# A hybrid layer on one core: ten ring tiles, square sums and scalings in quarters, and the first transfer on another queue

## The chip, the cores and the metric

The kernel runs on one core of a Trainium2 chip. The metric is the device time of one execution in microseconds (us); below, times inside the profiled execution count from the start of its span. TensorE (PE) multiplies, VectorE (DVE) and ScalarE (ACT) do element-wise work, GpSimd (POOL) does small work and issues its own transfers, SyncE (SP) issues transfers only. Each engine works through its instructions in order, and an instruction that waits holds all behind it.

## The reference

One layer over 256 rows of 2048 numbers, with two branches, all in float32:

```python
h = rms_norm(x, norm_g)
q, k, v, z_a, u_b, v_b, z_b, g_a, g_b = split(h @ w_in)      # 1024 columns each, g_a and g_b 2048
q, k = rms_norm of each head of 128, times its gain           # 8 heads
att = causal softmax attention(q, k, v)                       # one block: 256 rows are one MoBA block
y_a = (att * silu(z_a)) @ w_proj_a
sgu = gelu(u_b) * (causal w_spatial @ rms_norm(gelu(v_b), sgu_norm_g) + b_spatial)
y_b = (sgu * silu(z_b)) @ w_proj_b
out = x + (sigmoid(g_a) * y_a + sigmoid(g_b) * y_b) @ w_out
```

The sums of squares that concern the change are those of q and k and of gelu(v_b), each over groups of 128 columns.

## The kernel before

The weights are laid out in HBM as 120 tiles of 1 MB, 128 partitions of 2048 numbers, and one tile is one step i. Steps 0 to 7 make q, 8 to 15 k, then v, za, vb, ub, zb in eights (up to 55); from 56 on each of four column groups c has eight steps of the gates (g) and four of the projections (proj, PSUM tiles y); steps 104 to 119 make the output. A number after a tile's name is its step: tl13 is the tile tl of step 13.

Every float32 product is made from halves of fewer bits: ScalarE casts raw to wh, DVE subtracts to get wl (raw - wh), and TensorE does three products with the high and low halves. A plain step takes 24 matmuls. Of the eight steps of a projection behind q, up to five are Strassen steps (function `strassen`), which need 21 matmuls, and in exchange three more blocks: DVE makes t (lines 172 to 174, three instructions), ScalarE its high half th (L175), DVE its low half tl (L177). One of the four blocks of such a step is the sum of two, and this sum is made by transfers: SyncE copies a 256 KB piece of the weights to a ring of HBM tiles (L130, `pre_copy`), GpSimd adds a second piece by a transfer that accumulates (L134, `pre_sum`), and SyncE loads the ring tile as the first quarter of raw (L141) and the other 768 KB from the weights (L122). raw has four buffers, wh, wl and th three, tl two and t one.

The orders of SyncE and GpSimd are those in which the program is written (`queues`), so copies, loads, sums and GpSimd's powers stand in a fixed row. The orders of TensorE, DVE and ScalarE are found from step 8 on by the scheduler of the language, with costs of its own; up to there DVE and ScalarE go by the program too.

The loop over steps issues load(i + 3), pre_copy(i + 8), pre_sum(i + 6) and the split of step i + 2, then the matmuls of step i, then what `at` has put down for this step: `at(s, fn, ...)` calls fn at step s. `sums` squares a projection on ScalarE in four tiles of 128 x 512 (m, c), four instructions each with a sum along 128 columns (junk, ss); `rsqrt` makes the mean on DVE (ms, L268) and takes the power -0.5 on GpSimd (rs, L269); for k, DVE multiplies rs once more (L406). `norm_qk` and `norm_v` scale on ScalarE, four instructions for each tile (L415, L423). The tiles k_c11, k_c12, k_h, k_c22 are the four tiles of k.

At the start xv (the norm's gain and the first 256 columns of x transposed), raw0 in pieces and the rest of x are issued by SyncE in this order.

Of the kernel before, what the change touches and what calls it, by code (L numbers as in the profile page):

```python
# [12 lines left out]
F32 = mybir.dt.float32  # L13
# [3 lines left out]
AF = mybir.ActivationFunctionType  # L17
ALU = mybir.AluOpType
AX = mybir.AxisListType

P = 128
S = 256
# [7 lines left out]
B = 512  # L30
# [20 lines left out]
NVEC = KT + 2 + H  # L51
# [20 lines left out]
def hybrid_layer_kernel(  # L72
# [9 lines left out]
    nc = tc.nc  # L82
# [7 lines left out]
    small = ctx.enter_context(tc.tile_pool(name="small", bufs=4))  # L90
    psum = ctx.enter_context(tc.tile_pool(name="psum", bufs=1, space=bass.MemoryType.PSUM))
    dram = ctx.enter_context(tc.tile_pool(name="dram", bufs=1, space=bass.MemoryType.DRAM))
# [4 lines left out]
    def u(name, dtype=F32):  # L97
        return unit.tile([P, B], dtype, tag="u", name=name)
# [11 lines left out]

    raw, wh, wl, th, tl = {}, {}, {}, {}, {}
    pre = {}
    ring = [dram.tile([P, B], F32, tag=f"ring{n}", name=f"ring{n}") for n in range(6)]

    def strassen(i):
        if i >= NG or G[i][0] != "quad" or G[i][1] == G[0][1]:
            return False
        name, c, kp = G[i][1:4]
        return kp in SK or (name in FIVE and kp == 4) or (name == "g" and c in SIX and kp == 5)

    def load_piece(i, a, b):
        nc.sync.dma_start(raw[i][:, a:b], w[i, :, a:b])  # L122

    def new_raw(i):
        raw[i] = wpool.tile([P, WORDS], F32, tag="raw", bufs=4, name=f"raw{i}")

    def pre_copy(i):
        if i < NG and strassen(i):
            pre[i] = ring[len(pre) % len(ring)]
            nc.sync.dma_start(pre[i], w[i, :, 0:B])  # L130

    def pre_sum(i):
        if i in pre:
            nc.gpsimd.dma_start(pre[i], w[i, :, B:2 * B], accum_op=ALU.add)  # L134
# [44 lines left out]
    X = {}  # L179

    def heads(ap):
        return ap.rearrange("p (h d) -> p h d", d=P)
# [3 lines left out]
    xv = u("xv")  # L186
# [7 lines left out]
                          xT[:, NVEC + p0 * S:NVEC + p1 * S].rearrange("p (k t) -> p k t", t=S))  # L194

    new_raw(0)
    nc.sync.dma_start(xv[:, 0:NVEC + S], xT[:, 0:NVEC + S])
    load_piece(0, 0, B)
    load_piece(0, B, 2 * B)
    load_x(1, 2)  # L200
# [47 lines left out]
    gain = const.tile([P, P], F32, name="gain")  # L248
# [14 lines left out]
    rstd = const.tile([P, 2], F32, name="rstd")  # L263
    ssum = const.tile([P, 2], F32, name="ssum")

    def rsqrt(dst, src, n, count):
        ms = small.tile([P, 8], F32, tag="ms", name="ms")
        nc.vector.tensor_scalar(ms[:, :n], src, 1.0 / count, EPS, op0=ALU.mult, op1=ALU.add)  # L268
        nc.gpsimd.tensor_tensor(dst, ms[:, :n], mhalf[:, :n], op=ALU.pow)  # L269
# [121 lines left out]
        return [[c11, c12], [h, c22]]  # L391


    def sums(C, name):
        for m in range(2):
            for c in range(2):
                ss = small.tile([P, 4], F32, tag="ss", bufs=8, name="ss")
                junk = u("junk")
                scale = rstd[:, m:m + 1] if name == "k" else 1.0
                for h in range(4):  # L400
                    nc.scalar.activation(junk[:, h * P:(h + 1) * P], C[m][c][:, h * P:(h + 1) * P], AF.Square,
                                         scale=scale, accum_out=ss[:, h:h + 1])
                rs = small.tile([P, 4], F32, tag="rs", bufs=8, name="rs")
                rsqrt(rs, ss, 4, P)
                if name == "k":
                    nc.vector.tensor_scalar(rs, rs, scale, None, op0=ALU.mult)  # L406
                X["rs", name, m, c] = rs

    def norm_qk(name):
        C = X[name]  # L410
        for m in range(2):
            for c in range(2):
                for h in range(4):
                    sl = C[m][c][:, h * P:(h + 1) * P]
                    nc.scalar.activation(sl, sl, AF.Copy, scale=X["rs", name, m, c][:, h:h + 1])  # L415

    def norm_v():
        C = X["vb"]
        for m in range(2):
            for c in range(2):  # L420
                for h in range(4):
                    sl = C[m][c][:, h * P:(h + 1) * P]
                    nc.scalar.activation(sl, sl, AF.Copy, scale=X["rs", "vb", m, c][:, h:h + 1])  # L423
                t = heads(C[m][c])
                nc.vector.tensor_tensor(t, t, gain[:, None, :].to_broadcast([P, 4, P]), op=ALU.mult)

    def func(name, fn):
        for m in range(2):
# [168 lines left out]
    def at(i, fn, *a):  # L597
        later.setdefault(i, []).append((fn, a))
# [7 lines left out]
    i0 = first["q", 0]  # L606
# [6 lines left out]
    at(i0 + 6, halves_f, "x")  # L613
    at(i0 + 8, halves_4)
    i0 = first["k", 0]
    at(i0 + 1, sums, None, "q")
    at(i0 + 3, norm_qk, "q")
    i0 = first["v", 0]
    at(i0 + 0, turn_qk, "q", None)
    at(i0 + 1, sums, None, "k")  # L620
    at(i0 + 3, norm_qk, "k")
    i0 = first["za", 0]
    at(i0 + 0, turn_qk, "k", None)
    at(i0 + 1, score, None)
    at(i0 + 2, softmax, 0)
    at(i0 + 2, softmax, 1)
    i0 = first["vb", 0]
    at(i0 + 0, turn_p, 0, None)
    at(i0 + 0, turn_p, 1, None)
# [4 lines left out]
    i0 = first["ub", 0]  # L634
    at(i0 + 0, turn_z, "za", None)
    at(i0 + 0, causal_mix)
    at(i0 + 1, func, "vb", AF.Gelu_apprx_tanh)
    at(i0 + 2, sums, None, "vb")
    at(i0 + 4, norm_v)
    i0 = first["zb", 0]  # L640
    at(i0 + 0, mix, None)
    at(i0 + 1, func, "ub", AF.Gelu_apprx_tanh)
# [1 line left out]
    i0 = first["g", 0]  # L644
# [35 lines left out]
    for i, (kind, name, c, kp, n) in enumerate(G):  # L680
        if i == 8:
            ordered.close()
        if i:
            load(i + 3)
        if i >= 1:
            pre_copy(i + 8)
            pre_sum(i + 6)
        split(i + 2, 2 if i < 2 else 1)
        if i < 4:
            split_x(i + 4)  # L690
        plain = i < 8
        if kind == "quad":
            if n == 0:
                if i and G[i - 1][0] == "quad":

                    E, L = L, E
                Lt = [bank(b, f"acc_{name}{c}_{j}") for j, b in enumerate(L[:3])]
                Et = None
            if len(Lt) == 3 and (plain or not strassen(i)):
                Lt.append(bank(L[3], f"acc_{name}{c}_3"))  # L700
            if strassen(i) and Et is None:
                Et = [bank(b, f"seven_{name}{c}_{j}") for j, b in enumerate(E)]
            if strassen(i):
                last = SK[-1] if name not in FIVE else 5 if name == "g" and c in SIX else 4
                f8 = "m" if name == "out" else "x"
                seven(Et, Lt, i, kp, kp == SK[0], kp == last, n > 0, *fac(name), X["Fh", f8], X["Fl", f8])
                if kp == last:
                    e = early(Et, f"{name}{c}", xres.get(c) if name == "out" else None)
            else:
                direct(Lt, *fac(name), i, kp, (n == 0, not direct22(i)), n == 7)  # L710
            if n == 7:
                if plain:
                    X[name] = [[u(f"{name}{m}{j}") for j in range(2)] for m in range(2)]
                    for j in range(4):
                        nc.scalar.activation(X[name][j // 2][j % 2], Lt[j], AF.Copy, scale=rstd[:, j // 2:j // 2 + 1])
                elif name == "out":
                    post_out(c, Lt, e)
                elif name == "g":
                    X["g", c] = final(Lt, e)
                    for m in range(2):  # L720
                        for j in range(2):
                            nc.scalar.activation(X["g", c][m][j], X["g", c][m][j], AF.Sigmoid, scale=rstd[:, m:m + 1])
                else:
                    X[name] = final(Lt, e)
        elif kind == "proj":
            if n % 2 == 0:
                Y = (Y if n else []) + [bank(E[n + m], f"y{n}_{c}{m}") for m in range(2)]
            z = ("za", "zb")[n // 2]

            def hl(k, m):  # L730
                return (X[z + "h"][:, k, m * P:(m + 1) * P], X[z + "l"][:, k, m * P:(m + 1) * P])

            mm_rows(Y[n // 2 * 2:], hl, i, None, 4 * (n % 2), n % 2 == 0, n % 2 == 1)
            if n == 3:
                merge(c, Y)
        for fn, a in later.pop(i, []):
            a = list(a)
            if fn is sums:
                a[0] = X[a[1]]
            elif a and fn in (turn_qk, score, turn_p, attend, turn_z, mix, turn_m):  # L740
                if a[-1] is None:
                    a[-1] = list(E)
                    if fn is turn_p and a[0] == 1:
                        a[-1] = [E[3], E[0], E[1]]
                    if fn is attend:
                        a[-1] = E[2 * a[0]:]
                elif a[-1] == "late":
                    a[-1] = E[2:4] + L[0:2]
                elif a[-1] == "L01":
                    a[-1] = L[0:2]  # L750
                elif a[-1] == "L23":
                    a[-1] = L[2:4]
                elif a[-1] == "L3":
                    a[-1] = L[3:4]
            fn(*a)
# [48 lines left out]
```

## Time and profile before

| | before |
|---|---|
| median of 3 runs | 670.8 us (667.85 to 671.66) |
| profiled execution, time | 668.79 us |
| its span | 667.1 us |
| TensorE busy | 653.7 us (98%), 2959 matmuls |
| DVE busy | 601.8 us (90%) |
| ScalarE busy | 432.3 us (65%) |
| GpSimd busy | 73.2 us (11%) |
| mean granted TensorE clock | 0.997 |
| DMA engines, mean | 249 GB/s; HBM traffic 295 GB/s over the span |

The profiled execution spends 1.69 us outside the span. A busy share counts matmuls as running until their modelled ends, so a TensorE that is busy all the time may still wait a little between them. In a row of the timeline the first two numbers are the start and the duration of an instruction, or from the start of the first to the end of the last of a merged group (x2, x16); a bracket at the end gives the idle time of the engine just before, and what ended it.

### The profile page before, as it was taken

The page shows a single profiled execution, that of the slowest core. Times are in us where ns is not written, and L with a number is a line of the kernel's source. Part 1 is how long each engine was busy: PE and PEld are TensorE (multiplying, and loading weights), DVE is VectorE, ACT ScalarE, POOL GpSimd, SP SyncE. Part 2 cuts the span into 40 slices and gives each one's busy share as a digit, 9 for nine tenths or more (in the row PEclk, how much of TensorE's full clock was granted, in tenths as well). Part 3 has the DMA queues.
Part 4 walks back from the last instruction along what each step waited for, and adds up shares of the span by engine and source line. Part 5 has one row for each costly group of instructions (what it writes and reads, how often), then busy time and mean ns, then how long its engine had stood idle before and what let it go on. Part 6 is the DMA issues. An engine that isn't in the chain of part 4 may idle for free.

```text
span 667.1 us, 8042 instructions
## 1 busy us (share of the span) xinstructions
PE 653.7 (98%) x2959; PEld 533.4 (80%) x2959; DVE 601.8 (90%) x587; ACT 432.3 (65%) x521; POOL 73.2 (11%) x85
## 2 busy tenths in 40 slices
PE   8999899999999999999999999999999999999997
PEld 4888678788888788888877887788788878888875
DVE  4779888999898999999998999979988998999896
ACT  7968949857877679685654755556555564754360
POOL 1110503101000305000001100100010000000000
PEclk9999989999999999999999999999999999999999
DMA  8998894789687858967658973995598599777841
GB/s 303 396 407 272 257 333 145 208 282 271 176 284 219 257 201 251 329 194 235 220 205 271 283 250 145 340 289 199 194 350 249 204 276 307 242 181 246 235 200 63
DMA packets 47703, 166.28 MB, mean 249 GB/s; under 512 B 5296, under 2 KB 5936, under 8 KB 40112
## 3 DMA queue, kind: packets, MB, share of 16 engines
q1 hardware_dynamic: 38016, 148.21, 60.2%
q0 software_dynamic: 8496, 15.47, 15.6%
q10 hardware_dynamic: 1152, 2.10, 1.0%
q8 instruction: 23, 0.38, 0.2%
q14 instruction: 16, 0.13, 0.0%
HBM read 163.66 MB, written 33.03 MB: 295 GB/s over the span
## 4 chain that ended last, share of the span: by engine, by line
PE 67%; DVE 13%; ACT 8%; DMA 6%; issue 4%; POOL 1%; SPq 0%; DVEq 0%; ACTq 0%; POOLq 0%
PE y L323 13%; PE acc_g L323 11%; PE seven_g L323 6%; DMA raw<-in_w 6%; PE acc_za L323 5%; PE acc_ub L323 4%; PE acc_zb L323 4%; PE acc_vb L323 4%; DVE wl L176 3%; ACT wh L149 3%; PE acc_out L323 3%; DVE wl L150 3%; DVE tl L177 3%; PE acc_v L323 2%; PE seven_zb L323 2%
## 5 line engine op out<-in xcount | busy, mean ns | idle before, releaser
L150 DVE TENSOR_TENSOR wl<-raw,wh 128x2048 fp32r<-128x2048 f32 (+2 forms) x69 | 140.2, 2039 | 21.3 <-ACT wh L149 21.3
L149 ACT CAST wh<-raw 128x2048 fp32r<-128x2048 f32 (+2 forms) x69 | 117.4, 1713 | 60.5 <-PE acc_g L323 19.5
L171 ACT CAST wh<-raw 128x2048 fp32r<-128x2048 f32 x59 | 112.6, 1914 | 61.5 <-issue 12.8
L176 DVE TENSOR_TENSOR wl<-raw,wh 128x2048 fp32r<-128x2048 f32 x59 | 134.8, 2286 | 6.6 <-ACT wh L171 6.4
L175 ACT CAST th<-t 128x1536 fp32r<-128x1536 f32 x59 | 87.5, 1483 | 59.5 <-DVE t L174 58.1
L177 DVE TENSOR_TENSOR tl<-t,th 128x1536 fp32r<-128x1536 f32 x59 | 103.9, 1760 | 5.2 <-ACT th L175 5.2
L134 POOL DMA_DIRECT2D ring<-in_w x59 | 49.0, 882 | 456.0 <-DMA ring<-in_w 438.4
L172 DVE TENSOR_TENSOR t<-raw 128x512 f32<-128x512 f32 x59 | 40.9, 693 | 10.0 <-DMA raw<-in_w 9.4
L173 DVE TENSOR_TENSOR t<-t,raw 128x512 f32<-128x512 f32 x59 | 40.6, 687 | 0.9
L174 DVE TENSOR_TENSOR t<-t,raw 128x512 f32<-128x512 f32 x59 | 40.4, 684 | 0.0
L323 PE MATMUL acc_g<-wh,xul 128*128 128x512 f32 x99 | 38.6, 390 | 0.0
L323 PE MATMUL acc_g<-wl,xuh 128*128 128x512 f32 x99 | 38.6, 389 | 0.0
L323 PE MATMUL acc_g<-wh,xuh 128*128 128x512 f32 x99 | 38.5, 389 | 0.0
L323 PE MATMUL acc_out<-wl,mh 128*128 128x512 f32 x72 | 28.2, 391 | 0.8 <-DVE wl L150 0.8
L323 PE MATMUL acc_out<-wh,mh 128*128 128x512 f32 x72 | 28.0, 390 | 0.0
L323 PE MATMUL acc_out<-wh,ml 128*128 128x512 f32 x72 | 28.0, 391 | 0.0
L323 PE MATMUL acc_q<-wh,xuh 128*128 128x512 f32 x64 | 25.1, 392 | 1.7 <-ACT wh L149 1.7
L323 PE MATMUL acc_q<-wl,xuh 128*128 128x512 f32 x64 | 25.3, 396 | 0.4 <-DVE wl L150 0.2
L323 PE MATMUL y<-wh,zbl 128*128 128x512 f32 x64 | 25.1, 392 | 0.0
L323 PE MATMUL y<-wh,zal 128*128 128x512 f32 x64 | 25.0, 390 | 0.0
L323 PE MATMUL acc_q<-wh,xul 128*128 128x512 f32 x64 | 25.0, 390 | 0.0
L323 PE MATMUL y<-wl,zah 128*128 128x512 f32 x64 | 24.9, 389 | 0.0
(542 smaller groups left out, 1586.7 us busy)
## 6 DMA issues: line engine op xcount, KB each, us to landing
raw<-in_w SPq DMA_DIRECT2D x57, 1024.0 KB, 7.3
raw<-in_w SPq DMA_DIRECT2D x59, 768.0 KB, 6.7
ring<-in_w SPq DMA_DIRECT2D x59, 256.0 KB, 7.9
ring<-in_w POOLq DMA_DIRECT2D x59, 256.0 KB, 7.6
raw<-ring SPq DMA_DIRECT2D x59, 256.0 KB, 4.6
raw<-in_w SPq DMA_DIRECT2D x7, 512.0 KB, 8.7
xnat<-in_x SPq DMA_DIRECT2D x2, 1024.0 KB, 15.5
xres<-in_x ACTq DMA_DIRECT2D x8, 256.0 KB, 3.7
```

The lines of the kernel that those rows point to most:

```text
L134: nc.gpsimd.dma_start(pre[i], w[i, :, B:2 * B], accum_op=ALU.add)
L149: nc.scalar.copy(h, r)
L150: nc.vector.tensor_tensor(l, r, f(h), op=ALU.subtract)
L171: nc.scalar.copy(wh[i], r)
L172: nc.vector.tensor_tensor(T2, r[:, 0:B], r[:, 2 * B:3 * B], op=ALU.add)
L173: nc.vector.tensor_tensor(T1, T2, r[:, B:2 * B], op=ALU.subtract)
L174: nc.vector.tensor_tensor(T3, T2, r[:, 3 * B:], op=ALU.add)
L175: nc.scalar.copy(th[i], t)
L176: nc.vector.tensor_tensor(wl[i], r, f(wh[i]), op=ALU.subtract)
L177: nc.vector.tensor_tensor(tl[i], t, f(th[i]), op=ALU.subtract)
L323: nc.tensor.matmul(acc, a, b, start=(start and n == 0), stop=(stop and n == 2))
```

## The change

Three things. The ring has ten tiles in place of six; for steps from 16 on, a step's copy is issued 11 steps ahead in place of 8 and its sum 8 ahead in place of 6. `sums` and the scalings do one quarter at a time: the quarters n = 0 to 3 are the tiles (0, 0), (1, 0), (0, 1), (1, 1), and quarter n is put down one step behind quarter n - 1. (The second softmax half is put down one step later as well.) And xv is issued by ScalarE's queue.

```diff
-    ring = [dram.tile([P, B], F32, tag=f"ring{n}", name=f"ring{n}") for n in range(6)]
+    ring = [dram.tile([P, B], F32, tag=f"ring{n}", name=f"ring{n}") for n in range(10)]
...
-    nc.sync.dma_start(xv[:, 0:NVEC + S], xT[:, 0:NVEC + S])
+    nc.scalar.dma_start(xv[:, 0:NVEC + S], xT[:, 0:NVEC + S])
...
+    QUARTERS = ((0, 0), (1, 0), (0, 1), (1, 1))
+
+    def sums(name, n):
+        m, c = QUARTERS[n]
+        C = X[name][m][c]
...
+        for h in range(4):
+            nc.scalar.activation(junk[:, h * P:(h + 1) * P], C[:, h * P:(h + 1) * P], AF.Square,
+                                 scale=scale, accum_out=ss[:, h:h + 1])
...
+    def norm(name, n):
+        m, c = QUARTERS[n]
+        C = X[name][m][c]
+        for h in range(4):
+            sl = C[:, h * P:(h + 1) * P]
+            nc.scalar.activation(sl, sl, AF.Copy, scale=X["rs", name, n][:, h:h + 1])
+        if name == "vb":
+            t = heads(C)
+            nc.vector.tensor_tensor(t, t, gain[:, None, :].to_broadcast([P, 4, P]), op=ALU.mult)
...
     i0 = first["k", 0]
-    at(i0 + 1, sums, None, "q")
-    at(i0 + 3, norm_qk, "q")
+    for n in range(4):
+        at(i0 + 1 + n, sums, "q", n)
+        at(i0 + 3 + n, norm, "q", n)
     i0 = first["v", 0]
     at(i0 + 0, turn_qk, "q", None)
-    at(i0 + 1, sums, None, "k")
-    at(i0 + 3, norm_qk, "k")
+    for n in range(4):
+        at(i0 + 1 + n, sums, "k", n)
+        at(i0 + 3 + n, norm, "k", n)
...
-    at(i0 + 2, softmax, 1)
+    at(i0 + 3, softmax, 1)
...
-    at(i0 + 2, sums, None, "vb")
-    at(i0 + 4, norm_v)
+    for n in range(4):
+        at(i0 + 2 + n, sums, "vb", n)
+        at(i0 + 4 + n, norm, "vb", n)
...
-        if i >= 1:
-            pre_copy(i + 8)
-            pre_sum(i + 6)
+        for j in range(i + 6, i + 12):
+            if j == i + (8 if j < 16 else 11):
+                pre_copy(j)
+            if j == i + (6 if j < 16 else 8):
+                pre_sum(j)
```

What this does to the orders of the engines is shown at three places.

ScalarE in the k projection, before. Here q00 to q11 are the four tiles of q, junk the target of the squares, and wh and th the casts of the weights:

```order
L401 ACTIVATE junk_609,ss_608<-q11_495 128x128 x4
L171 CAST wh12_623<-raw12_546 128x2048
L175 CAST th12_625<-t12_622 128x1536
L171 CAST wh13_660<-raw13_618 128x2048
L415 ACTIVATE q00_492<-q00_492,rs_584 128x128 x4
L415 ACTIVATE q01_493<-q01_493,rs_594 128x128 x4
L415 ACTIVATE q10_494<-q10_494,rs_604 128x128 x4
L415 ACTIVATE q11_495<-q11_495,rs_614 128x128 x4
L171 CAST wh14_716<-raw14_655 128x2048
L175 CAST th13_662<-t13_659 128x1536
```

ScalarE at the same place after the change:

```order
L171 CAST wh12_601<-raw12_552 128x2048
L403 ACTIVATE junk_634,ss_633<-q10_499 128x128 x4
L416 ACTIVATE q00_497<-q00_497,rs_591 128x128 x4
L403 ACTIVATE junk_689,ss_688<-q01_498 128x128
L171 CAST wh13_649<-raw13_595 128x2048
L175 CAST th12_603<-t12_600 128x1536
L403 ACTIVATE junk_689,ss_688<-q01_498 128x128 x3
L416 ACTIVATE q10_499<-q10_499,rs_639 128x128 x4
L403 ACTIVATE junk_739,ss_738<-q11_500 128x128 x4
L416 ACTIVATE q01_498<-q01_498,rs_694 128x128 x4
L171 CAST wh14_702<-raw14_643 128x2048
L175 CAST th13_651<-t13_648 128x1536
```

Squares and scalings now alternate, with the casts of the weights between them; wh14 still stands ahead of th13, and the scalings of q11 have moved behind wh15, below this piece. The squares of q00 stand above the piece in both, and ahead of wh12 after the change.

DVE in the v projection, before:

```order
L172 TENSOR_TENSOR t20_1007<-raw20_920 128x512
L406 TENSOR_SCALAR rs_998<-rs_998,rstd_138 128x4
L173 TENSOR_TENSOR t20_1007<-t20_1007,raw20_920 128x512
L174 TENSOR_TENSOR t20_1007<-t20_1007,raw20_920 128x512
L176 TENSOR_TENSOR wl20_1009<-raw20_920,wh20_1008 128x2048
L177 TENSOR_TENSOR tl20_1011<-t20_1007,th20_1010 128x1536
L176 TENSOR_TENSOR wl21_1050<-raw21_1003,wh21_1049 128x2048
L172 TENSOR_TENSOR t21_1048<-raw21_1003 128x512
L173 TENSOR_TENSOR t21_1048<-t21_1048,raw21_1003 128x512
L174 TENSOR_TENSOR t21_1048<-t21_1048,raw21_1003 128x512
L176 TENSOR_TENSOR wl22_1102<-raw22_1044,wh22_1101 128x2048
L177 TENSOR_TENSOR tl21_1052<-t21_1048,th21_1051 128x1536
```

DVE at the same place after the change:

```order
L172 TENSOR_TENSOR t20_981<-raw20_926 128x512
L176 TENSOR_TENSOR wl20_983<-raw20_926,wh20_982 128x2048
L173 TENSOR_TENSOR t20_981<-t20_981,raw20_926 128x512
L174 TENSOR_TENSOR t20_981<-t20_981,raw20_926 128x512
L176 TENSOR_TENSOR wl21_1036<-raw21_976,wh21_1035 128x2048
L177 TENSOR_TENSOR tl20_985<-t20_981,th20_984 128x1536
L176 TENSOR_TENSOR wl22_1086<-raw22_1029,wh22_1085 128x2048
L172 TENSOR_TENSOR t21_1034<-raw21_976 128x512
L268 TENSOR_SCALAR ms_1128<-ss_1121 128x4
L173 TENSOR_TENSOR t21_1034<-t21_1034,raw21_976 128x512
L174 TENSOR_TENSOR t21_1034<-t21_1034,raw21_976 128x512
L408 TENSOR_SCALAR rs_1127<-rs_1127,rstd_142 128x4
```

wl21 stands ahead of tl20 now, and wl23 and then tl21 follow behind the last row of this piece; the last multiplication of rs has moved from the second row behind t21.

GpSimd at that place, before (rs is the power, ring the accumulating transfer of a sum):

```order
L269 TENSOR_TENSOR rs_965<-ms_966,mhalf_129 128x4
L269 TENSOR_TENSOR rs_976<-ms_977,mhalf_129 128x4
L269 TENSOR_TENSOR rs_987<-ms_988,mhalf_129 128x4
L269 TENSOR_TENSOR rs_998<-ms_999,mhalf_129 128x4
L134 DMA ring4_81<-in_w 128x512
```

GpSimd at that place after the change:

```order
L269 TENSOR_TENSOR rs_971<-ms_972,mhalf_133 128x4
L134 DMA ring0_77<-in_w 128x512
L269 TENSOR_TENSOR rs_1024<-ms_1025,mhalf_133 128x4
L134 DMA ring1_78<-in_w 128x512
L269 TENSOR_TENSOR rs_1077<-ms_1078,mhalf_133 128x4
L269 TENSOR_TENSOR rs_1127<-ms_1128,mhalf_133 128x4
L134 DMA ring2_79<-in_w 128x512
```

Two sums now stand between the powers of k.

SyncE in the second column group of gates and projections, before:

```order
L122 DMA raw76_3447<-in_w 128x2048
L130 DMA ring3_80<-in_w 128x512
L122 DMA raw77_3475<-in_w 128x2048
L130 DMA ring4_81<-in_w 128x512
L122 DMA raw78_3512<-in_w 128x2048
L130 DMA ring5_82<-in_w 128x512
L122 DMA raw79_3552<-in_w 128x2048
L130 DMA ring0_77<-in_w 128x512
L122 DMA raw80_3586<-in_w 128x2048
L130 DMA ring1_78<-in_w 128x512
L141 DMA raw81_3618<-ring3_80 128x512
L122 DMA raw81_3618<-in_w 128x1536
```

SyncE at the same place after the change:

```order
L122 DMA raw76_3454<-in_w 128x2048
L130 DMA ring2_79<-in_w 128x512
L122 DMA raw77_3483<-in_w 128x2048
L130 DMA ring3_80<-in_w 128x512
L122 DMA raw78_3521<-in_w 128x2048
L130 DMA ring4_81<-in_w 128x512
L122 DMA raw79_3561<-in_w 128x2048
L122 DMA raw80_3594<-in_w 128x2048
L141 DMA raw81_3625<-ring9_86 128x512
L122 DMA raw81_3625<-in_w 128x1536
```

The six copies for this group begin three steps earlier, right behind the load of raw73, and none stands between raw79 and raw81 any more.

## Rows read from the trace of the kernel before

**Rows 1.** The page's first part: busy us and share, and the number of instructions, of each engine; the line begins with TensorE and its weight loads.

```profile
PE 653.7 (98%) x2959; PEld 533.4 (80%) x2959; DVE 601.8 (90%) x587; ACT 432.3 (65%) x521; POOL 73.2 (11%) x85
```

**Rows 2.** The list of waits, of TensorE: the waiting group, what it waited for, us in total, times, the longest.

```profile
PE seven_k L323 <- DVE tl L177: 1.9, 1, 1.9
PE acc_q L323 <- ACT wh L149: 1.7, 1, 1.7
...
PE seven_g L323 <- ACT th L175: 0.9, 1, 0.9
PE seven_g L323 <- DVE tl L177: 0.9, 2, 0.6
...
PE seven_vb L323 <- DVE tl L177: 0.4, 1, 0.4
```

**Rows 3.** The timeline of TensorE in the k projection, around its two longest waits.

```profile
79.50 0.39 PE L323 MATMUL seven_k<-wl,Fhx 128*128 128x512 f32 x1
80.55 0.50 PE L323 MATMUL seven_k<-th,Flx 128*128 128x512 f32 x1 [0.67 <-ACT th L175]
...
83.18 0.50 PE L323 MATMUL seven_k<-tl,Fhx 128*128 128x512 f32 x1 [1.89 <-DVE tl L177]
83.51 0.43 PE L323 MATMUL seven_k<-th,Flx 128*128 128x512 f32 x1
83.74 0.63 PE L323 MATMUL seven_k<-th,Fhx 128*128 128x512 f32 x1
...
87.15 0.39 PE L323 MATMUL acc_k<-wh,xul 128*128 128x512 f32 x1
```

**Rows 4.** Stretches of 2 us behind them, TensorE alone: the stretch, its length, TensorE's busy us (instructions), the granted clock, the DMA share, GB/s.

```profile
84.00:86.00 2.00, 2.00 (x6) 0.50 1.04 269
86.00:88.00 2.00, 2.00 (x8) 0.71 0.92 262
```

**Rows 5.** The timeline of the start, all engines.

```profile
0.80 0.38 SPq L197 DMA_DIRECT2D xv<-in_xT  x1
...
1.24 0.89 SPq L122 DMA_DIRECT2D raw<-in_w  x2
...
5.83 1.29 ACT L149 CAST wh<-raw 128x512 fp32r<-128x512 f32 x2 [1.83 <-DMA raw<-in_w]
...
6.50 0.50 PE L323 MATMUL acc_q<-wh,xuh 128*128 128x512 f32 x1 [1.65 <-ACT wh L149]
```

**Rows 6.** The timeline of the k projection on GpSimd, ScalarE (wh of step 11, the 16 scalings of q, wh of step 14, th of step 13) and DVE (wl of step 14, tl of step 13).

```profile
66.32 6.31 POOL L269 TENSOR_TENSOR rs<-ms,mhalf 128x4 f32<-128x4 f32 x4 [15.93 <-DVE ms L268]
...
61.63 1.94 ACT L149 CAST wh<-raw 128x2048 fp32r<-128x2048 f32 x1
...
72.53 4.80 ACT L415 ACTIVATE q<-q,rs 128x128 f32<-128x128 f32 x16
77.22 1.91 ACT L171 CAST wh<-raw 128x2048 fp32r<-128x2048 f32 x1
79.01 1.49 ACT L175 CAST th<-t 128x1536 fp32r<-128x1536 f32 x1
...
79.16 2.29 DVE L176 TENSOR_TENSOR wl<-raw,wh 128x2048 fp32r<-128x2048 f32 x1 [1.59 <-ACT wh L171]
81.37 1.75 DVE L177 TENSOR_TENSOR tl<-t,th 128x1536 fp32r<-128x1536 f32 x1
```

**Rows 7.** The timeline of the v projection: on DVE the third multiplication of rs, the last t and wl and tl of step 20, tl of step 21; two sums of GpSimd; TensorE's first use of tl20 and of th21.

```profile
112.76 0.23 DVE L406 TENSOR_SCALAR rs<-rs,rstd 128x4 f32<-128x4 f32 x1 [1.12 <-POOL rs L269]
...
117.01 0.69 DVE L174 TENSOR_TENSOR t<-t,raw 128x512 f32<-128x512 f32 x1
117.61 2.29 DVE L176 TENSOR_TENSOR wl<-raw,wh 128x2048 fp32r<-128x2048 f32 x1
119.81 1.75 DVE L177 TENSOR_TENSOR tl<-t,th 128x1536 fp32r<-128x1536 f32 x1
...
127.96 1.75 DVE L177 TENSOR_TENSOR tl<-t,th 128x1536 fp32r<-128x1536 f32 x1
...
116.20 1.74 POOL L134 DMA_DIRECT2D ring<-in_w  x2
...
122.85 0.39 PE L323 MATMUL seven_v<-tl,Fhx 128*128 128x512 f32 x1
...
127.28 0.50 PE L323 MATMUL seven_v<-th,Flx 128*128 128x512 f32 x1
```

**Rows 8.** The gates. The timeline: the second part of raw81 on SyncE, the first t made of it on DVE, TensorE's wait for tl of step 84. Then two stretches with all engines (TensorE, weight loads, DVE, ScalarE, GpSimd busy us with instructions; then clock, DMA share, GB/s). Then two lines of SyncE's list of waits.

```profile
426.91 0.43 SPq L122 DMA_DIRECT2D raw<-in_w  x1
...
440.44 0.69 DVE L172 TENSOR_TENSOR t<-raw 128x512 f32<-128x512 f32 x1 [4.24 <-DMA raw<-in_w]
...
476.07 0.73 PE L323 MATMUL seven_g<-tl,Fhx 128*128 128x512 f32 x2 [0.62 <-DVE tl L177]
...
440.40:476.10 35.70, 35.08 (x156) 28.73 (x154) 35.52 (x31) 20.94 (x12) 0.81 (x1) 1.00 0.63 206
500.00:560.00 60.00, 59.85 (x263) 48.81 (x263) 56.02 (x50) 32.55 (x23) 4.09 (x5) 1.00 0.80 260
...
SPq L122 <- DVE t L174: 119.1, 25, 11.2
...
SPq L141 <- DMA ring<-in_w: 41.0, 14, 8.8
```

More of the change, by code (lines that the diff above doesn't have):

```diff
@@ L391, in final @@
         return [[c11, c12], [h, c22]]
[L394 to L425, printed above, removed]
+    QUARTERS = ((0, 0), (1, 0), (0, 1), (1, 1))
@@ new lines, in sums @@
+    def sums(name, n):
+        m, c = QUARTERS[n]
+        C = X[name][m][c]
+        ss = small.tile([P, 4], F32, tag="ss", bufs=8, name="ss")
+        junk = u("junk")
+        scale = rstd[:, m:m + 1] if name == "k" else 1.0
+        for h in range(4):
+            nc.scalar.activation(junk[:, h * P:(h + 1) * P], C[:, h * P:(h + 1) * P], AF.Square,
+                                 scale=scale, accum_out=ss[:, h:h + 1])
+        rs = small.tile([P, 4], F32, tag="rs", bufs=8, name="rs")
+        rsqrt(rs, ss, 4, P)
+        if name == "k":
+            nc.vector.tensor_scalar(rs, rs, scale, None, op0=ALU.mult)
+        X["rs", name, n] = rs
@@ L737, in hybrid_layer_kernel @@
             a = list(a)
-            if fn is sums:
-                a[0] = X[a[1]]
-            elif a and fn in (turn_qk, score, turn_p, attend, turn_z, mix, turn_m):
+            if a and fn in (turn_qk, score, turn_p, attend, turn_z, mix, turn_m):
                 if a[-1] is None:
```

## The prediction

> **What bounds the kernel now.** First the busy time: TensorE works 653.7 us, 98% of the span [rows 1], so what the other engines can win by another order is at most the missing 13 us and what TensorE does slowly. Then TensorE's list of waits: no entry is over 1.9 us [rows 2]. The reader is to see in it where a change can pay: the k projection, the first weight tile (1.7), the gates (0.9 + 0.9), one place in vb (0.4). What an idle stretch costs is a little more than its wait: ahead of the matmul at 80.55 the wait is 0.67, but from the start at 79.50 to it are 1.05 us where warm matmuls follow one another every 0.23 us (83.51 to 83.74), so 0.82 are lost, 0.15 more than the wait [rows 3]. And in k a third cost stands behind the two waits: ten matmuls from 83.74 to 87.15 start 0.42 to 0.43 us apart instead of 0.23, with a granted clock of 0.50 in 84 to 86 and 0.71 in 86 to 88 [rows 3, 4]; that is (0.425 - 0.227) x 8 to 10 = 1.6 to 2.0 us. So the k stall costs 0.82 + 2.04 + about 1.8 = 4.7 us and is the largest prize.
>
> **The start.** Before, xv is issued at 0.80 on SyncE and the first 256 KB of raw0 at 1.24; they land in time for ScalarE's cast at 5.83 and the first real matmul at 6.50 [rows 5]. Without xv ahead of it, raw0 and everything behind it in SyncE's queue go 1.24 - 0.80 = 0.44 us sooner. ScalarE, which issues xv now, has nothing else that must be done before raw0 has landed but the work on xv itself. If landing follows issue, the gain is 0.44; if the two transfers now share the engines while both run, it is nothing. I take -0.3 (0 to -0.45). The Trainium skill (DMA: Bandwidth & Descriptors, "Queues, rings and completion order") says that each DMA engine takes turns between queue rows, packet by packet; by that rule xv would run beside raw0 in place of ahead of it and this term would be near 0. No row of before shows two hardware queues at the start.
>
> **The k projection.** tl13 is late because of a chain in ScalarE's order: 16 scalings of q from 72.53 to 77.22, then wh14, then DVE's wl14, which starts at 79.16 when wh14 is done, and tl13 behind it at 81.37 [rows 6]. After, the order still puts wh14 and wl14 ahead of th13 and tl13; only 4 of the 16 scalings (4.69 / 16 = 0.29 each, 1.2 us) go behind th13. Against that, ScalarE now waits for GpSimd inside its order. GpSimd's four powers took 6.31 us in a row from 66.32 [rows 6], 1.6 each. Before, the first scaling came after all of them. After, the first four scalings stand behind wh12 and the squares of the second quarter. From wh11 at 61.63: two casts of 1.8 and six squares, taken like scalings at 0.29, bring ScalarE there at 67.0, while the first power, started as before at 66.3, ends at 67.9: a wait of 0.9. Five of 0.29 and wh13 later it is 71.2. The third quarter's ms stands on DVE behind wl13 (2.2) and tl12 (1.7), which end at 75.1, so its power ends at 76.7, while ScalarE is done with th12 (1.4) and eleven squares and scalings at 75.8 and waits 0.9 again. Its four scalings end at 77.9, and wh14 starts there instead of at 77.22. So th13 and tl13 come 0.6 later; the slow clock stays (1.8 before and after), and as th14 moves ahead of the k copy and wh17 about 0.3 comes back later. I take +0.3, between -1.2 (no power waited for) and +0.9. The Trainium skill (TensorE: Matmul & The Clock Gate, "What's actually happening") wants an idle window of some 3.4 us before the clock halves. Here it halved although two matmuls, those of the stretch from 80.55, ran in the 3.4 us from 79.7 to 83.18 [rows 3, 4], so the rows put the limit a little lower than the page; by the page a v stage that waits for about 1 us at a time keeps its clock, and by the rows that is open, which is rival (b).
>
> **The v projection.** The squares of k go into four parts too, and GpSimd's order now has ring sums between the powers. Each sum takes 0.87 to issue (1.74 for two) [rows 7]. Before, the third rs multiplication of DVE was at 112.76; two sum issues ahead of its power put it about 1.3 later, at 114.05, and with it tl19 and t20. Then DVE's order itself is worse: wl21 stands ahead of tl20 and wl23 ahead of tl21, at 2.2 each (117.61 to 119.81). From 114.05: tl19 1.67, t20 0.61, wl20 2.20, t20 1.21, wl21 2.20, tl20 1.75 gives 123.7, against 121.56 before [rows 7]. TensorE wants it at 122.85: a wait of about 0.85. On: wl22 2.20, three t21 and ms 1.95 (0.60 each, 0.15) give 127.95; th21 (1.4) ends at 129.4 where TensorE, 0.85 late, wants it at 127.28 + 0.85 = 128.1: 1.3. The rs multiplication and wl23 come first, so tl21 ends at 132.1, against 129.71 before [rows 7]. At that point v is about 2.4 late. What DVE is ahead with, wl23 and the next t, comes off its work behind tl21, and I let that make good 0.6, an estimate. I take +1.8, with 0 (the powers not delayed, 1.3 taken off every step, and slack at th21) and +2.6 as its bounds.
>
> **vb and the softmax.** One wait of vb, 0.4 + 0.15 [rows 2], falls away, as after asks for tl38 five matmuls later: -0.5 (0 to -0.5). The vb scalings in parts and the later softmax stand on ScalarE and DVE among splits that TensorE doesn't wait for in that stretch before, since its list names nothing there but the one place; cost 0, covered by that lead, and at worst one power, 1.6.
>
> **The gates.** A ring copy 11 steps ahead in place of 8 moves DMA from one place to another. In gate 1, the copies stand between the loads of raw76 to raw81; raw81, whose second part is issued at 426.91, comes for DVE at 440.44, 13.5 us later; DVE waits 4.24 for it and then works without a break (35.52 of 35.70 us) to tl84, which is late by 0.62 at 476.07 [rows 8]. After, the copies for 82 to 86 stand behind raw74 to raw78, ending before raw79, and raw81 has the engines to itself but for earlier sums. If it comes 1 us sooner, that wait is gone; I expect 3. The same shape recurs in gates 2 and 3. To be had: the two waits for tl of 0.9 together (the longer the one at 476.07) and twice 0.15, and 60.00 - 59.85 + 0.15 = 0.30 in 500 to 560 [rows 2, 8], together 1.5. The other 0.9, for th in gate 0, hangs on raw65, behind which a copy still stands, and is left. I take -1.5; with slots of raw as the limit (below) it would be 0.
>
> **Sum.** -0.3 + 0.3 + 1.8 - 0.5 - 1.5 = -0.2 on a span of 667.1. With the 668.79 - 667.1 = 1.7 outside the span, the profiled run would be 668.6. The median of before is 670.8, 2.0 above its profiled run, so on the same footing 670.6; I say 670.5.
>
> **Rivals.** (a) Faster: the quarters do what they read as. ScalarE is not held by a power, wh14 comes 1.2 sooner, the wait at tl13 falls below 1 us and the clock isn't lowered (-1.2 - 1.8), v costs nothing, start, vb and gates as above: -0.3 - 3.0 - 0.5 - 1.5 = -5.3, about 665.5. For it: the scalings do fill ScalarE for 4.7 us right ahead of wh14. Against: wh14 and wl14 still stand first. (b) Slower: v is where it goes wrong. If TensorE waits twice for over 1 us near 123 to 132, as in k, the clock falls there as well: +2.6 + 1.8, k +0.9, gates 0, vb 0, start 0: +5.3, or 676; it decides once tl20 and tl21 come over 2 us late. Against it: no such fall behind the waits in the gates, where the clock is 1.00 from 440 to 476 and from 500 to 560 [rows 8]. (c) Slower: a power stands behind a sum whose copy hasn't landed. SyncE and GpSimd keep their orders, and sums waited 41.0 us in 14 cases for loads from the ring [rows 8]; one such hold of 4 us stops ScalarE and DVE in k or v: +4, 674.6. Against it: copies go 8 steps ahead where q is normed. (d) The DMA part does nothing: SyncE's loads wait mostly for DVE to free raw (119.1 us in 25 cases for t alone) [rows 8], so raw81 is issued no sooner and lands no sooner: +1.3, 672.1, no change that can be told.
>
> **Chances.** Forecast 0.40, (a) 0.30, (b) 0.11, (c) 0.05, (d) 0.14. A measurement of this kernel can tell 0.5%, 3.35 us, from no change; forecast and (d) lie within, so same 0.54, faster 0.30, slower 0.16. The forecast's own range is 668 to 673. For 8 in 10 it reaches to (a), 665.5, and one us below it for its spread, and short of (b): 664.5 to 674.5.
>
> **What would show it.** Start: first real matmul at 6.2. k: wh14 still ahead of th13, a wait for tl13 of about 2 us and a clock of 0.5 behind it; no such clock means (a). v: TensorE waits for tl20, th21 and tl21, all three absent before or under 0.4. Gates: DVE's waits for raw of 4 us shrink and TensorE's for tl go. A low clock in v, or ScalarE's idle time put down to GpSimd by more than 2 us, would make the forecast too low; wh14 before 76 would make it too high.

## The result and the profile after

The changed kernel takes 671.83 us (median of 20 runs, 670.65 to 674.15), the kernel before 667.87 (20 runs beside it): a ratio of 1.0059 with a 95% interval of 1.0045 to 1.0073. It is slower by about 4 us. The forecast was no change (670.5, with a sum of -0.2 us), and it is wrong: the change costs time. The profiled execution of after took 671.31 with a span of 669.6, against 668.79 and 667.1 before.

TensorE's list of waits of after (columns as in [rows 2]):

```profile
PE seven_k L323 <- DVE tl L177: 3.8, 2, 1.9
PE seven_k L323 <- ACT th L175: 2.4, 2, 1.5
PE acc_q L323 <- ACT wh L149: 1.8, 1, 1.8
...
PE seven_v L323 <- ACT th L175: 1.0, 1, 1.0
PE seven_v L323 <- DVE tl L177: 1.0, 1, 1.0
...
PE acc_out L323 <- DVE wl L150: 0.3, 1, 0.3
...
```

Set beside [rows 2], the gates and vb have left the list, and in k the wait for tl of 1.9, which came once before, comes twice now; its waits for th have gone from 0.7 to 2.4. v is new with 1.0 and 1.0.

To compare stretches, the tables below use one number for TensorE, its loss: by how much the starts of successive matmuls of one stretch lie further apart than the 0.227 us of warm matmuls, summed over the timeline. It holds waits, restarts and slow clock alike.

| loss in us, by stretch | 0-25 | 25-100 (q, k) | 100-150 (v) | 150-325 | 325-575 (gates) | 575-end | sum |
|---|---|---|---|---|---|---|---|
| before | 3.6 | 4.9 | 1.8 | 1.6 | 4.2 | 2.0 | 18.0 |
| after | 2.7 | 10.1 | 2.9 | 1.7 | 1.6 | 1.5 | 20.5 |

The sums differ by 2.5 us, as the two spans of these profiled executions do. The gates gave 2.6 back, k took 5.2 and v 1.1. So the question is k. There, the timeline of after, GpSimd first, then ScalarE (scalings of q00, wh13, th12), then DVE (the first t12, wl12, the last t12, wl13), then TensorE's four waits:

```profile
66.43 4.82 POOL L269 TENSOR_TENSOR rs<-ms,mhalf 128x4 f32<-128x4 f32 x1 [15.93 <-DVE ms L268]
...
71.28 1.28 ACT L416 ACTIVATE q<-q,rs 128x128 f32<-128x128 f32 x4 [4.07 <-POOL rs L269]
...
72.76 1.90 ACT L171 CAST wh<-raw 128x2048 fp32r<-128x2048 f32 x1
74.56 1.47 ACT L175 CAST th<-t 128x1536 fp32r<-128x1536 f32 x1
...
66.25 0.68 DVE L172 TENSOR_TENSOR t<-raw 128x512 f32<-128x512 f32 x1
66.85 2.28 DVE L176 TENSOR_TENSOR wl<-raw,wh 128x2048 fp32r<-128x2048 f32 x1
...
69.66 0.68 DVE L174 TENSOR_TENSOR t<-t,raw 128x512 f32<-128x512 f32 x1
...
74.69 2.29 DVE L176 TENSOR_TENSOR wl<-raw,wh 128x2048 fp32r<-128x2048 f32 x1 [4.26 <-ACT wh L171]
...
76.08 0.50 PE L323 MATMUL seven_k<-th,Flx 128*128 128x512 f32 x1 [0.87 <-ACT th L175]
...
78.71 0.50 PE L323 MATMUL seven_k<-tl,Fhx 128*128 128x512 f32 x1 [1.89 <-DVE tl L177]
...
84.81 0.50 PE L323 MATMUL seven_k<-th,Flx 128*128 128x512 f32 x1 [1.50 <-ACT th L175]
...
87.44 0.79 PE L323 MATMUL seven_k<-tl,Fhx 128*128 128x512 f32 x1 [1.89 <-DVE tl L177]
```

A power of 128 x 4 numbers takes 4.82 us. It starts at 66.43, 0.18 after DVE has begun t12, and it ends at 71.25, 0.9 after the last long DVE instruction of an unbroken row (69.66 + 0.68 = 70.34). ScalarE, in order, waits 4.07 us for it ahead of the scalings, so wh13 starts at 72.76, and DVE waits 4.26 us for wh13. From there everything in k is late, at step 12 already and at step 13 again.

### The profile page after: what moved, and what is told of

Its sections match the earlier page's. It is cut to its first block, busy times and chain, and to the rows that moved or that the text cites. A ratio compares the mean times of both kernels' runs of the same rounds, so it can differ in the third digit from the quotient of the medians.

```text
span 669.6 us, 8030 instructions
## 1 busy us (share of the span) xinstructions
PE 652.9 (98%) x2959; PEld 533.5 (80%) x2959; DVE 601.4 (90%) x587; ACT 431.7 (64%) x521; POOL 74.2 (11%) x85
## 4 chain that ended last, share of the span: by engine, by line
PE 68%; DVE 10%; issue 10%; ACT 5%; DMA 4%; POOL 2%; DVEq 0%; SPq 0%; ACTq 0%; POOLq 0%
PE acc_g L323 14%; PE y L323 13%; PE seven_g L323 9%; PE acc_ub L323 4%; PE acc_za L323 4%; PE acc_vb L323 4%; DMA raw<-in_w 4%; PE acc_zb L323 3%; PE acc_out L323 3%; DVE wl L150 3%; ACT wh L149 2%; DVE wl L176 2%; DVE tl L177 2%; PE seven_vb L323 2%; PE seven_ub L323 2%
## 5 line engine op out<-in xcount | busy, mean ns | idle before, releaser
L134 POOL DMA_DIRECT2D ring<-in_w x59 | 50.8, 903 | 409.3 <-DMA ring<-in_w 406.5
L269 POOL TENSOR_TENSOR rs<-ms,mhalf 128x4 f32<-128x4 f32 x12 | 21.9, 1822 | 88.8 <-DVE ms L268 88.8
```

## The experiments

Each run was timed beside the kernel before, on the same chip; "ratio" is to that, with its 95% interval behind it. The losses are of one profiled execution each.

**The parts alone.** First, xv alone:

```diff
-    nc.sync.dma_start(xv[:, 0:NVEC + S], xT[:, 0:NVEC + S])
+    nc.scalar.dma_start(xv[:, 0:NVEC + S], xT[:, 0:NVEC + S])
```

> The kernel before with xv alone moved to ScalarE's queue. Theory: in the trace of after, xv lands 2.1 us later, the first matmul comes 0.16 later, and yet TensorE loses 0.9 less by 25 us; so alone it gives -0.9 us (ratio about 0.9985), first matmul at 6.6 to 6.7. Rival: the smaller loss by 25 us was due to something else in after; then alone it gives +0.2 or nothing.

Measured: 667.53 us, ratio 1.000 (0.9985 to 1.0015). The theory falls; the move of xv gives nothing that can be told, and 1 us either way is what can be told here. ScalarE's first use of xv before, and then this run's start:

```profile
3.06 0.51 ACT L230 ACTIVATE xt<-xv 128x256 f32<-128x256 f32 x1 [0.98 <-DMA xv<-in_xT]
...
0.81 0.40 ACTq L197 DMA_DIRECT2D xv<-in_xT  x1
5.05 0.51 ACT L230 ACTIVATE xt<-xv 128x256 f32<-128x256 f32 x1 [2.53 <-DMA xv<-in_xT]
...
6.57 0.50 PE L323 MATMUL acc_q<-wh,xuh 128*128 128x512 f32 x1 [2.06 <-ACT wh L149]
```

xv is now ready some 4.2 us after its issue (0.81 to 5.05), where it took 2.3 before (0.80 to 3.06). The first real matmul starts at 6.57, no earlier than in [rows 5].

The ring alone (`range(6)` to `range(10)`, and the new rule for pre_copy and pre_sum):

> The kernel before with the ten ring tiles and the longer lead alone. Theory: the gates' waits for tl go, as in after: -1.5 to -2.0 us (ratio 0.997 to 0.9985). Rival (the lead is what costs: more sums and copies beside the loads of k and v): no gain, or slower by up to 2 us, with waits in k or v that the kernel before does not have.

Measured: 665.15 us, ratio 0.9969 (0.9955 to 0.9983). Loss in k and v 3.5 and 1.8, neither higher than before. The longer lead is a gain and not the cause.

The quarters alone (the new `sums` and `norm`, their steps, the later softmax half):

> The kernel before with the square sums and scalings in quarters (and the later softmax half) alone. Theory (GpSimd's power of a quarter now runs beside DVE's long subtraction and is held by it, ScalarE waits in order): +5 to +7 us (ratio 1.008 to 1.0105), first power of q near 4.8 us long, ScalarE waits 4 us for it, TensorE waits twice in k, some 9 us lost in k against 4.8. Rival (the power is late through the ring sums that the longer lead brings): without the longer lead the first power takes under 2 us and the ratio is within 1.003.

Measured: 675.47 us, ratio 1.013 (1.0109 to 1.0151), loss 9.3 in 25 to 100 and 4.9 in v; the first power of q takes 4.82 without any longer lead. It costs more than was expected. The whole loss of the change sits in the quarters, and more than the whole.

After without the quarters:

> After without the quarters: ten ring tiles, longer lead, xv on ScalarE's queue, sums and scalings as before. Theory: the two gains add, -2.4 to -2.9 us (ratio 0.9955 to 0.9965), the fastest so far. Rival: gains that come out one by one do not add, -1 or less.

Measured: 664.65 us, ratio 0.9961 (0.9945 to 0.9978). It beats both kernels.

**Which quarters.** After, with q whole:

```diff
-        at(i0 + 1 + n, sums, "q", n)
-        at(i0 + 3 + n, norm, "q", n)
+        at(i0 + 1, sums, "q", n)
+        at(i0 + 3, norm, "q", n)
```

> After, with the sums and scalings of q whole again (all four at the steps at which before has them); k and vb stay in quarters. Theory (the held power of q's first quarter is what makes k slow): TensorE's loss in k falls from about 10 us back to about 5, the ratio to before from 1.006 to 0.998 (0.996 to 1.000), and the waits in v stay. Rival (the k part goes wrong through the ring's lead): loss in k stays near 10, ratio 1.004 or more.

Measured: 672.72 us, ratio 1.0064 (1.0038 to 1.0091). A miss: k's loss did fall, 10.1 to 6.2, but the time did not. TensorE's list in this run:

```profile
PE seven_v L323 <- ACT th L175: 3.7, 3, 2.1
...
PE seven_v L323 <- DVE tl L177: 0.8, 1, 0.8
```

What was taken out of k has come up in v: a loss of 7.3 there against 2.9 in after. But DVE's order in v is not that of after. The scheduler has found another, in which wl20 stands ahead of tl19 and wl21 ahead of all of t20. The timeline (wl20, tl19, wl21, the first t20):

```profile
115.90 2.29 DVE L176 TENSOR_TENSOR wl<-raw,wh 128x2048 fp32r<-128x2048 f32 x1
118.11 1.75 DVE L177 TENSOR_TENSOR tl<-t,th 128x1536 fp32r<-128x1536 f32 x1
119.78 2.29 DVE L176 TENSOR_TENSOR wl<-raw,wh 128x2048 fp32r<-128x2048 f32 x1
121.98 0.68 DVE L172 TENSOR_TENSOR t<-raw 128x512 f32<-128x512 f32 x1
```

So this run does not tell what k's quarters cost in after.

The same with k whole too, so that only vb and the softmax differ from the last kernel of the parts:

> After, with the sums and scalings of q and of k whole again; vb stays in quarters. Theory (v's waits of 1.2 and 1.2 in after come from k's quarters): TensorE's loss in 100 to 150 us falls from 2.9 to 1.8 or less, the ratio to before is 0.996 (0.9945 to 0.9975). Rival (v's waits come from the ring's lead or are carried over from the late k): they stay, and this run is no faster than the one with only q whole.

Measured: 665.36 us, ratio 0.9954 (0.9932 to 0.9977), loss in v 1.8 as before. The quarters of vb and the later softmax cost nothing that can be told; k's, with the order that came with them, made the difference between 1.0064 and 0.9954.

**The held power.** After with one more DVE instruction for each quarter of q:

```diff
+        if name == "q":
+            nc.vector.tensor_scalar(rs, rs, 1.0, None, op0=ALU.mult)
```

> After, with one added multiplication of rs by 1.0 on DVE for each quarter of q, which by the order stands ahead of the long subtraction wl12, so that DVE waits for the power and leaves it alone. Nothing else is meant to change; scalings of q move a little. Theory (the power is held by DVE): the first power of q falls from 4.8 to 1.0 to 1.7 us, ScalarE's wait of 4.1 to about 1, TensorE's loss in k by 3 to 5 us, ratio to before 0.999 to 1.002. Rival (the first power is long in itself, or held by something on GpSimd): it stays near 4.8, now DVE waits for it too, ratio 1.006 or more.

Measured: 669.80 us, ratio 1.0021 (1.0001 to 1.0041); the first power 1.40 us, the loss in 25 to 100 down from 10.1 to 4.6, that in v up from 2.9 to 4.3. In v, DVE's order around steps 19 to 21 is that of after, apart from one short instruction, and TensorE now comes there on time. It waits for tl20, th21 and tl21:

```profile
123.48 0.50 PE L323 MATMUL seven_v<-tl,Fhx 128*128 128x512 f32 x1 [1.23 <-DVE tl L177]
129.12 0.50 PE L323 MATMUL seven_v<-th,Flx 128*128 128x512 f32 x1 [1.01 <-ACT th L175]
132.01 0.74 PE L323 MATMUL seven_v<-tl,Fhx 128*128 128x512 f32 x2 [1.00 <-DVE tl L177]
```

So this run shows best what k's quarters cost when TensorE is not late. The loss of 4.3 in v stands against 1.8 in before, and against 2.8 in the last run of the next pair, which differs by having k, vb and the softmax whole: 1.5 to 2.5 us.

The cleaner pair has k, vb and softmax whole, and q in quarters without and with that instruction.

> Ring of ten, longer lead, xv on ScalarE's queue, and q alone in quarters (k, vb and the softmax as before). Theory (the held power of q's first quarter): first power 4.8 us, ScalarE waits 4 us for it, TensorE's loss in 25 to 100 us near 10 as in after, v's loss not much above before's 1.8; ratio to before 1.001 to 1.004. Rival (q's quarters cost little once k's are whole, as with q whole the time did not fall): ratio 0.997 or less.

> The same with the multiplication by 1.0 on DVE behind each power of q, which keeps DVE off the first power. It differs from the other in these four small instructions and what the scheduler moves for them. Theory: the first power takes 1.4, TensorE's loss in 25 to 100 us is near 4.6, ratio to before 0.994 to 0.998, 0.5 to 0.8% under the other. Rival (the hold is not what costs): the two are within 0.2% of each other.

Measured: 669.77 us, ratio 1.0036 (1.0020 to 1.0051) without, and 666.24, ratio 0.9986 (0.9969 to 1.0003) with it. The timeline without (GpSimd, ScalarE):

```profile
66.23 4.82 POOL L269 TENSOR_TENSOR rs<-ms,mhalf 128x4 f32<-128x4 f32 x1 [15.93 <-DVE ms L268]
...
71.08 1.28 ACT L416 ACTIVATE q<-q,rs 128x128 f32<-128x128 f32 x4 [4.05 <-POOL rs L269]
```

and with it (GpSimd's first two powers, DVE, ScalarE):

```profile
65.45 1.40 POOL L269 TENSOR_TENSOR rs<-ms,mhalf 128x4 f32<-128x4 f32 x1 [15.92 <-DVE ms L268]
...
70.64 3.12 POOL L269 TENSOR_TENSOR rs<-ms,mhalf 128x4 f32<-128x4 f32 x1 [2.94 <-DVE ms L268]
...
66.89 0.17 DVE L410 TENSOR_SCALAR rs<-rs 128x4 f32<-128x4 f32 x1 [0.93 <-POOL rs L269]
66.97 2.29 DVE L176 TENSOR_TENSOR wl<-raw,wh 128x2048 fp32r<-128x2048 f32 x1
...
67.15 1.28 ACT L418 ACTIVATE q<-q,rs 128x128 f32<-128x128 f32 x4 [0.89 <-DVE rs L410]
```

Four added instructions, and a DVE that stands still for 0.93 us, make the kernel 0.5% faster, because wl12 now starts behind the power and not beside it. ScalarE waits 0.89 in place of 4.05. Up to wh13 its order is the same in both runs, and wh13 starts at 68.63 in place of 72.56, where wh12 was only 0.75 ahead; behind wh13 the scheduler has moved some scalings as well. The hold is the cause in k. It has not gone altogether: the second power, beside wl13, takes 3.12, and the ratio stays 0.25% above the 0.9961 of the kernel without quarters, hardly more than the intervals.

The power by itself, in a kernel that computes no layer:

> No layer is computed here: the output is zeros and the weights but for one tile aren't read. Powers of 128x4 alone on GpSimd, twice each: with DVE idle; beside two DVE subtractions of 128x2048; beside eight DVE additions of 128x512; beside six of 128x512 with one operand in PSUM; beside two multiplications by a constant of 128x2048; beside two ScalarE casts of 128x2048. Theory (held by DVE's two-operand instructions): about 1.0 with DVE idle and beside ScalarE, 3 to 5 beside the 2048 subtractions, less beside the 512s. Rival (no hold): about 1.0 in all six.

The timeline of GpSimd (without its sixth power, act, at 24.07), of DVE in the stretches with work, and of ScalarE's casts:

```profile
5.98 1.01 POOL L129 TENSOR_TENSOR idle<-ms,mhalf 128x4 f32<-128x4 f32 x1 [5.14 <-DVE ms L128]
7.48 2.98 POOL L129 TENSOR_TENSOR tt<-ms,mhalf 128x4 f32<-128x4 f32 x1 [0.49 <-DVE ms L128]
12.29 1.38 POOL L129 TENSOR_TENSOR tt_512x<-ms,mhalf 128x4 f32<-128x4 f32 x1 [1.82 <-DVE ms L128]
17.38 1.01 POOL L129 TENSOR_TENSOR ps_512x<-ms,mhalf 128x4 f32<-128x4 f32 x1 [3.71 <-DVE ms L128]
21.24 2.35 POOL L129 TENSOR_TENSOR ts<-ms,mhalf 128x4 f32<-128x4 f32 x1 [2.86 <-DVE ms L128]
7.31 4.61 DVE L108 TENSOR_TENSOR dst<-src,a 128x2048 f32<-128x2048 f32 x2
...
17.21 3.67 DVE L116 TENSOR_TENSOR dst<-src,ps 128x512 f32<-128x512 f32 x6
...
21.07 2.48 DVE L119 TENSOR_SCALAR dst<-src 128x2048 f32<-128x2048 f32 x2
...
7.55 7.69 ACT L122 COPY adst<-src 128x2048 f32<-128x2048 f32 x4
```

The second round repeats it to the hundredth. With DVE idle the power takes 1.01. Beside a subtraction of 128x2048 from two SBUF tiles it takes 2.98, and beside one-operand multiplications of that size 2.35. Beside additions of 128x512 from two SBUF tiles it takes 1.38, and beside additions of the same size with one operand in PSUM 1.01, although DVE is busy throughout. So it is neither DVE's being busy nor the power itself, but what DVE reads, and how long its instructions are. The part with ScalarE missed its aim: all four casts ran from 7.55 to 15.24 and none beside the sixth power. But they did run beside the second and third, and these took the same 2.98 and 1.38 in the second round without any cast: ScalarE makes no difference to them.

The Trainium skill (SBUF — State Buffer, "SBUF: two separate sides") says this: GpSimd and DVE share a pair of ports, which an instruction takes as a whole, DVE's with two SBUF inputs among them, and the loser is blocked. The runs agree where GpSimd is the loser. Where DVE should be, they do not: the second subtraction starts at 9.63, beside the last 0.8 us of the power, and the two together take 4.61 us, no more than twice 2.28 with 0.04 between.

One thing stays open. In the kernel the power was held over several DVE instructions in a row, 4.82 us; here it came through after the first, even in the unbroken row of 128x512 additions.

**k's powers.** After with q whole, and k's sums and powers whole too, its scalings still in quarters:

> After with q whole, and of k the squares and powers whole too; only the scalings of k (and vb) stay in quarters. Now no ring sum stands between the powers of k, and DVE makes tl20 before wl21 as in before, while wl22 stays ahead of the end of t21. Theory (with k's powers between ring sums, DVE and ScalarE wait in a row, which costs v 5.5 us when k is on time): TensorE's loss in 100 to 150 us falls from 7.3 to 1.8 to 3, ratio to before 0.995 to 0.998. Rival (the scalings in quarters cost v its time): loss 6 or more, ratio 1.003 or more.

Measured: 666.73 us, ratio 0.9986 (0.9971 to 1.0002), loss in v 2.3 against 7.3 with k's powers in quarters. In GpSimd's timeline k's powers come ahead of the sums again:

```profile
108.02 2.46 POOL L269 TENSOR_TENSOR rs<-ms,mhalf 128x4 f32<-128x4 f32 x2 [25.44 <-DVE ms L268]
...
115.37 2.59 POOL L134 DMA_DIRECT2D ring<-in_w  x3
```

So the 5 us that v lost with q whole are not due to k's scalings in quarters. They are due to its squares and powers in quarters, or to the order that the scheduler found with them: this edit also brings tl19 back ahead of wl20 and t20 ahead of wl21, and the two were not taken apart.

**The gain without its powers.** After without the quarters, with the scalings of q put down two steps later (`at(i0 + 5, norm_qk, "q")`):

> Ten ring tiles, longer lead, xv on ScalarE's queue, sums whole; the scalings of q are put down two steps later, and by the order this takes only the last four of them from ahead of wh14 to behind wh15. This is what the prediction thought of as the gain of the quarters without their powers. Theory: wh14 starts 1.2 us earlier, TensorE's wait for tl13 falls from 1.9 to about 0.8, and the slow clock behind it shrinks or goes; 1 to 2.5 us under the same kernel without it, ratio to before 0.9925 to 0.9955. Rival (wh14's start hangs on raw14 or on DVE): the wait stays, ratio 0.996.

Measured: 666.15 us, ratio 0.9980 (0.9965 to 0.9995), a miss: not faster than 0.9961 without it. The timeline (ScalarE's wh14, TensorE's wait for tl13) and then the list of TensorE's waits:

```profile
75.57 1.90 ACT L171 CAST wh<-raw 128x2048 fp32r<-128x2048 f32 x1
...
81.52 0.50 PE L323 MATMUL seven_k<-tl,Fhx 128*128 128x512 f32 x1 [1.11 <-DVE tl L177]
```

```profile
PE seven_v L323 <- DVE tl L177: 1.5, 2, 0.8
...
PE acc_v L323 <- DVE wl L176: 1.2, 1, 1.2
...
```

wh14 does start 1.2 us earlier (75.57 against 76.81) and the wait for tl13 falls from 1.9 to 1.1. But a wait of 1.0 for a later th follows in k, and 1.2 and 1.5 in v, where the loss is 4.1 against 1.8. What was won in k is given back; why v's tiles come later there was not traced.

| kernel | ratio | loss 25-100 | loss 100-150 | loss 325-575 |
|---|---|---|---|---|
| xv alone | 1.000 | 4.0 | 1.9 | 2.9 |
| ring alone | 0.9969 | 3.5 | 1.8 | 2.8 |
| ring and xv | 0.9961 | 2.6 | 1.8 | 1.8 |
| quarters alone | 1.013 | 9.3 | 4.9 | 2.8 |
| ring, xv, q in quarters | 1.0036 | 7.9 | 1.4 | 2.5 |
| the same, DVE waits | 0.9986 | 4.3 | 2.8 | 1.4 |
| after, q whole | 1.0064 | 6.2 | 7.3 | 2.1 |
| after, q and k whole | 0.9954 | 5.8 | 1.8 | 2.1 |
| after | 1.0059 | 10.1 | 2.9 | 1.6 |

## Why the prediction was wrong

**k, the step that failed.** "the first power, started as before at 66.3, ends at 67.9". It started at 66.43 and ended at 71.25. The duration, 6.31 / 4 = 1.6 [rows 6], was an average over four powers of 1.50, 1.29, 1.00 and 2.59 us. The fourth began while wl13 ran, and ended 0.87 after it (GpSimd, DVE, in the kernel before):

```profile
70.05 2.59 POOL L269 TENSOR_TENSOR rs<-ms,mhalf 128x4 f32<-128x4 f32 x1
...
69.48 2.29 DVE L176 TENSOR_TENSOR wl<-raw,wh 128x2048 fp32r<-128x2048 f32 x1 [1.17 <-ACT wh L171]
```

So the trace of before already had a power held by a long subtraction. After, wl12 and the three t12 lay beside the first, which before had only t12 beside it and took 1.50. (That it came through behind wl13 before, although tl12 followed at once, and not behind wl12 after, is the point left open above.) The step before it was right (ScalarE was there at 67.1, 66.81 + 0.3), and so was the form of what follows: a wait of ScalarE, 4.07 in place of 0.9, and a second one, 1.05 for 0.9. With 3.2 us more, the term of +0.3 became +5.2 in loss, since step 12 is late as well: before, its tl was ready 2.0 us ahead of its use and no more. Rival (c) had the right victim, a power that holds ScalarE, at nearly the right price of 4, and the wrong holder: the first power stands ahead of the sums, and no copy was late. The prediction's own sign for "too low" was ScalarE waiting for GpSimd by more than 2 us; it waited 5.1.

**v.** +1.8 forecast, +1.1 in after by the loss; the waits for th21 and tl21 came as forecast (1.04 and 1.00), that for tl20 did not, as TensorE was later than DVE by then. Where k is nearly on time and DVE's order the same (after with DVE waiting for q's powers), all three waits are there, 1.23, 1.01 and 1.00, where the forecast had 0.85 for tl20 and 1.3 for th21, and v loses 1.5 to 2.5 more than without k's quarters. So the mechanism holds, and its size of 1.8 is about right. (One sum of this paragraph of the prediction is off by 0.1: 123.7 + 2.20 + 1.95 is 127.85. It changes nothing.) The order that the scheduler finds counts for more than the term: the one with q whole cost 7.3 - 1.8 = 5.5, of which 2.1 is a single wait for a th that stands behind a cast held 2.90 by a late load. In the kernel as changed, the quarters of q cost 0.75% (1.0036 - 0.9961), and those of k 0.23% on top (1.0059 - 1.0036), each good to some 0.2%.

**The start.** -0.3 forecast, first real matmul at 6.2; it came at 6.57, and no gain in time could be told. The alternative the prediction named is what the timeline shows: xv, on its own queue, takes 4.2 us in place of 2.3 and raw0 is not sooner. The Trainium skill's rule of turns between queues (DMA: Bandwidth & Descriptors, "Queues, rings and completion order") would make it so, and no run contradicts it.

**The gates.** -1.5 forecast, -2.6 by the loss. The wait for th in gate 0, which was written off, has gone too; the gain hoped for in 500 to 560 has not come. TensorE's busy time in 350 to 420, before and after (columns as in [rows 8]):

```profile
350.00:420.00 70.00, 68.78 (x309) 55.98 (x308) 65.75 (x61) 41.12 (x30) 5.76 (x7) 1.00 0.74 241
...
350.00:420.00 70.00, 70.00 (x316) 57.48 (x315) 67.48 (x64) 43.52 (x32) 6.25 (x8) 1.00 0.80 251
```

In 420 to 500 it is 80.00 against 79.38, and in 500 to 560 59.87 against 59.85.

Rival (d) is refuted by this and by the ring alone at 0.9969. vb's wait went, as forecast.

**The footing.** The 2.0 us between profiled run and median came from three runs; with 20 the median of before is 667.87, 0.9 below the profiled run. So this footing made the forecast 2.9 us too high, and the term for k made it 4.9 too low: that 670.5 is close to 671.83 is luck.

**The slow clock** was taken as a fixed price of the stall, 1.8. It isn't fixed: in the ring-and-xv kernel the same wait for tl13, 1.89 at 82.77, is followed by a full clock:

```profile
82.00:84.00 2.00, 1.24 (x5) 1.00 1.07 317
84.00:86.00 2.00, 2.00 (x10) 1.00 0.93 150
```

against 0.50 in 84 to 86 in [rows 4]. xv alone had it slow (0.51); the ring alone had it full, although its two waits in k, 0.7 and 1.9, are those of before. So what the prediction read out of [rows 3, 4] about the idle time after which the clock falls is not borne out; what decides it was not found. With one profile each, up to 1.8 of the differences in loss by 100 us is this.

## What to carry to other kernels

A short GpSimd instruction in a chain of dependent work costs what DVE does beside it: read its longest duration in the trace and what ran on DVE then, not its mean, before an order is changed that puts long two-operand DVE work next to it. Here the longest, 2.59 us, stood in the trace of before. Where the result is wanted soon, let DVE wait for it: 0.93 us of DVE bought 3.3 us (0.5%) of the kernel. And time the parts of a change apart, on an otherwise good kernel; here one part gave 0.3 to 0.4% and another took 1%. Then look at the orders in each such run: with q whole the scheduler found another one for v, and that run could not tell what the rest of the change costs.

## What the runs showed of the hardware that was not expected

A power of 512 numbers on GpSimd takes 1.01 us alone and up to 4.82 beside DVE; an operand in PSUM on DVE's side leaves it at 1.01, one-operand DVE instructions of 128x2048 do not (2.35). A subtraction of DVE's that began beside a power was not lengthened by it (4.61 us for two). A transfer of 141 KB, issued from a second hardware queue at the same time as two of 256 KB, was ready 4.2 us after its issue, and 2.3 us after it when issued alone 0.44 us ahead of them. And the same stall of 1.89 us was followed by half of TensorE's clock in some profiles and by the full clock in others.
